# Forget gates of a decoder trunk: from 24 split products on 16 lanes to 32 single precision products in four column tiles

## The chip, the cores and the metric

The kernel runs on one core of a Trainium2 chip. A core has five engines that run their own instruction streams beside each other: PE (TensorE, matrix products into PSUM), DVE (VectorE), ACT (ScalarE), POOL (GpSimd) and SP (SyncE, which here only issues DMAs). PE's work shows as two kinds of records, loads of the stationary operand (PEld) and products (PE). The metric is the device time of one execution in microseconds; smaller is better.

## The reference, cut to what matters

The model is a trunk of two layers over 512 tokens of width 1024. Layer 0 is a dilated attention with a convolutional feed-forward network (FFN). After it, keys, values and one forget gate for each of 16 heads are projected once from the residual stream; layer 1 is a causal attention over them, with a bias made of the gates, and a second FFN. The gates are the part that the change touches:

```python
kvf = rms_norm(h, kv_norm) @ w_kvf                       # (1, 512, 2064)
k_sh = kvf[..., :B_WIDTH].reshape(B, T, B_HEADS, HEAD_DIM)
v_sh = kvf[..., B_WIDTH:2 * B_WIDTH].reshape(B, T, B_HEADS, HEAD_DIM)
log_f = jax.nn.log_sigmoid((kvf[..., 2 * B_WIDTH:] + b_f).astype(jnp.float32))
c_sh = jnp.cumsum(log_f, axis=1)                         # over the 512 tokens
...
s = s + (c_t[:, :, q0:q1, None] - c_t[:, :, None, :q1])  # in the cross attention
```

Everything is single precision (float32) and the result is compared at that precision. The gates are a product of 512 x 1024 by 1024 x 16, a bias, a log of a sigmoid, and a running sum over tokens.

## The kernel before

*Split products.* Nearly all products of the kernel are made of three: each float32 operand is split into a high part, rounded to the matrix engine's fast type float32r, and a low part, the rest; high by high, high by low and low by high are added up in PSUM (`mm3`, lines 263 to 266: L264, L265 and L266 are these three). The class `Weights` (L33) loads pieces of the weights through SP's queue (L47), rounds them on ACT (L55) and subtracts on DVE (L63); `W.get` hands out the next pair and splits a few pieces ahead of use.

*Layout.* Activations lie transposed: 128 of the 1024 features on the partitions, 8 chunks of them, and the 512 tokens along the free dimension. `SharedBoundary` (L432) stands between the FFN of layer 0 and the shared projections. For each block of 128 tokens it normalizes a row block, transposes it on PE (L468), scales it by the gain of `kv_norm` (L470, `gcol`), and keeps it three ways: `xT` high (L475, ACT) and low (L476, DVE), both scaled, and `nT` (L480, ACT), the transposed input without a gain, in float32. `second` (L486, L487) makes the queries' input from `nT` with the other gain.

*The stage around the gates.* The order of the instructions of each engine is the order in which the program issues them. After the first half of the values (`values`, `keep_values`) a loop over 8 chunks of 128 key features runs: `keys(c)` multiplies a weight piece by `xT` (24 products into `k_ps`), ACT keeps the high half (L1299), DVE the low (L1300); for the first four chunks two chunks of the queries' input are made as well. In the rounds 1 to 5 the loop also calls `next(gate)`, one step of the generator `gates`: round 1 issues the products and ACT's copy with the bias, rounds 2 to 4 the chain of the log of the sigmoid, round 5 the running sum `c8`. In round 6 SP writes `c8` to memory (`cd`), from which `load_ck` later reads it back, spread over the partitions. After the loop PE transposes `c8` (`cq_ps`), the second half of the values follows, and then the cross attention, whose biases POOL makes of `ck` and `cq`.

*The products of the gates.* The weights of the gates (1024 x 16) are loaded and split ahead of the first FFN, at L1274 to L1278, their bias at L1280. `gates` multiplies 16 columns of weights by 512 tokens, 8 chunks in three products each, into one PSUM bank of 16 partitions (`f_ps`); the chain runs on tiles of 16 partitions by 512 tokens.

*Column tiles.* PE's array has 128 columns, one for each output partition. A product with few columns can be put into a part of it; the partition at which its output begins says which. The cross attention's products with the values (L1537, `o_ps`) do so with two halves of 64, one for each head of a pair; the gates of before use the first 32 columns only.

Of the kernel before, what the change touches and what calls it, by code (L numbers as in the profile page):

```python
# [8 lines left out]
F32 = mybir.dt.float32  # L9
F32R = mybir.dt.float32r  # L10
BF16 = mybir.dt.bfloat16
AF = mybir.ActivationFunctionType
ALU = mybir.AluOpType

D = 1024
T = 512
NB = 4
KD = D // 128
# [79 lines left out]
def trunk_kernel(ctx, tc, x, norm_gains, w_qkv_a, w_o_a, w_q_b, w_o_b, kv_norm, w_kvf, b_f,  # L98
                 w_up, conv_w, conv_b, w_down, rope, out):
    nc = tc.nc  # L100
    act, dve, pool, pe, sp = nc.scalar, nc.vector, nc.gpsimd, nc.tensor, nc.sync
# [5 lines left out]
    sml = ctx.enter_context(tc.tile_pool(name="sml", bufs=6))  # L107
# [8 lines left out]
    def t2(shape, dt=F32, name="t2"):  # L116
        return p2.tile(shape, dt, tag="t2", name=name)

    def bank(shape, name="bank"):
        return psp.tile(shape, F32, tag="ps", name=name)  # L120
# [86 lines left out]
    def load_gain(src, name):  # L207
        t = t4([128, D], name=name)
        sp.dma_start(t, bass.AP(tensor=src.tensor, offset=src.offset, ap=[[0, 128], [1, D]]))
        return t  # L210
# [52 lines left out]
    def mm3(o, ah, al, bh, bl, first, last, shared=False):  # L263
        pe.matmul(o, ah, bh, start=first, stop=False, skip_group_check=shared)  # L264
        pe.matmul(o, ah, bl, start=False, stop=False, skip_group_check=shared)  # L265
        pe.matmul(o, al, bh, start=False, stop=last, skip_group_check=shared)  # L266
# [71 lines left out]
    def xs(xT, kc, s):  # L338
        return xT[0][kc // 4][:, kc % 4, s], xT[1][kc // 4][:, kc % 4, s]
# [8 lines left out]
    ALL, LO, HI = slice(0, 512), slice(0, 256), slice(256, 512)  # L348
# [909 lines left out]
    gcol = sml.tile([128, 16], F32, tag="gcol", name="gcol", bufs=1)  # L1258
# [13 lines left out]

    wf = t2([128, 8, 16], name="wf")
    sp.dma_start(wf, w_kvf[:, 2048:2064].rearrange("(k p) c -> p k c", p=128))  # L1274
    wfh = sml.tile([128, 8, 16], F32R, tag="wfh", name="wfh", bufs=1)
    wfl = sml.tile([128, 8, 16], F32R, tag="wfl", name="wfl", bufs=1)
    dve.tensor_copy(wfh, wf)
    dve.tensor_tensor(wfl, wf, wfh.bitcast(F32), ALU.subtract)  # L1278
    bfc = sml.tile([16, 1], F32, tag="bfc", name="bfc", bufs=1)
    sp.dma_start(bfc, b_f.rearrange("(p o) -> p o", o=1))  # L1280


    bd2 = SharedBoundary(load_gain(norm_gains[0, 3], "gain03"), gcol, "xk")
# [18 lines left out]
    c8 = t2([16, T], name="c8")  # L1302

    def gates():

        fo = bank([16, T], name="f_ps")
        for s in (ALL,):
            for kc in range(KD):
                bh, bl = xs(bd2.xT, kc, s)
                mm3(fo[:, s], wfh[:, kc, :], wfl[:, kc, :], bh, bl, kc == 0, kc == KD - 1)  # L1310

        z = t2([16, T], name="z")
        act.activation(z, fo, AF.Identity, bias=bfc)
        yield
        u = t2([16, T], name="u")
        e = t2([16, T], name="e")
        dve.tensor_scalar(u, z, -1.0, None, ALU.mult)
        dve.tensor_tensor(u, u, z, ALU.min)
        act.activation(e, u, AF.Exp)
        yield  # L1320
        dve.tensor_scalar(u, e, 1.0, None, ALU.add)
        dve.scalar_tensor_tensor(e, u, -1.0, e, ALU.add, ALU.subtract)
        dve.tensor_scalar(z, z, 0.0, None, ALU.min)
        lg = t2([16, T], name="lg")
        act.activation(lg, u, AF.Ln)
        dve.reciprocal(u, u)
        yield
        dve.tensor_tensor(e, e, u, ALU.mult)
        dve.tensor_tensor(lg, lg, e, ALU.subtract)
        dve.tensor_tensor(z, z, lg, ALU.subtract)  # L1330
        dve.memset(u, 1.0)
        yield
        dve.tensor_tensor_scan(c8, u, z, 0.0, ALU.mult, ALU.add)
        dve.tensor_scalar(c8, c8, 8.0, None, ALU.mult)
        yield

# [19 lines left out]
    first, second = bd2.order[:2], bd2.order[2:]  # L1356
    bd2.norm(second[1])
    gate = gates()
    banks = {b: bank([128, 512], name="v_ps") for b in bd2.order}
    wv = []  # L1360
# [115 lines left out]
    def f_scores(j, i0):  # L1476

        if i0 == 0:
            o = [bank([128, 2, 256], name="s_ps") for _ in range(2)]
            s = [[o[hh][:, i] for hh in range(2)] for i in range(2)]  # L1480
        else:
            s = [[bank([128, T], name="s_ps") for _ in range(2)] for _ in range(2)]
        q, k = query_parts(j), key_parts(j)
        for i in range(2):
            nn = max((i0 + i + 1) * 128, 256)
            qs = slice((i0 + i) * 128, (i0 + i + 1) * 128)
            for n, (a, b) in enumerate(((0, 0), (1, 0), (0, 1))):
                for hh in range(2):
                    rows = slice(64 * hh, 64 * hh + 64)
                    pe.matmul(s[i][hh][:, :nn], q[a][rows, qs], k[b][rows, :nn], start=n == 0, stop=n == 2)  # L1490
        return s
# [73 lines left out]
    for m in range(M + 2):  # L1565
        live = m < M
        if live:
# [3 lines left out]
            s = f_scores(j, i0)  # L1571
# [11 lines left out]
        for a in range(2):  # L1583
            i = i0 + a
# [72 lines left out]
```

## Time and profile before

| | us |
|---|---|
| median of 3 runs | 1122.44 |
| lowest and highest of them | 1122.23, 1122.62 |
| the profiled execution, its time | 1124.33 |
| the profiled execution, its span from first to last instruction | 1122.1 |
| granted clock of TensorE in it | 0.997 of full |

| stage | us from the span's start |
|---|---|
| gates' weights and bias issued on SP | 171 |
| first key product | 552 |
| products of the gates | 563.0 to 568.6 |
| ACT's copy of them with the bias | 568.8 |
| running sum `c8` done | 594.9 |
| first product of the cross attention with the values | 643.1 |

How to read the rows that follow: in the timeline the first two numbers are the start and the duration in us, then engine, line, operation, output<-inputs, shape and count; several of a kind in a row are merged into one, with the whole stretch as duration. For a product, "128*16" is rows by columns of the array in use, and "128x512" its streamed input, partitions by elements. Both float32 and float32r are written f32 there. In brackets stands how long the engine was idle before, and what ended that. SPq is SP's queue, where issues of DMAs stand. In views by line, three numbers with slashes are the least, median and greatest duration in ns. In a view of windows, the busy us of PE, PEld, DVE, ACT and POOL follow with their counts, then the granted clock, the share of the DMA engines and GB/s.

### The profile page before, as it was taken

What the parts mean: (1) busy time and instruction counts of PE and PEld (TensorE: products, weight loads), DVE (VectorE), ACT (ScalarE), POOL (GpSimd) and SP (SyncE); (2) the same over time, 40 slices, a digit from 0 to 9 for tenths busy, and PEclk for the clock granted to TensorE, in tenths of its full rate; (3) what the DMA queues carried; (4) which work ended last, traced back from release to release, by engine and by line L of the source; (5) the groups of instructions that cost most, each with busy time, mean ns of one, the idle gap of its engine ahead of it and who ended that gap; (6) DMA issues with size and microseconds to landing.
All of it is one profiled execution on the core that took longest, in us unless ns stands there. A gap on an engine that the chain in (4) does not pass through costs nothing.

```text
span 1122.1 us, 17314 instructions
## 1 busy us (share of the span) xinstructions
PE 1111.5 (99%) x6331; PEld 946.1 (84%) x6331; DVE 876.5 (78%) x1433; ACT 606.2 (54%) x1022; POOL 181.1 (16%) x275
## 2 busy tenths in 40 slices
PE   9999999999999999999999999999999999999997
PEld 6988789989989988888878788889989989988886
DVE  6667778888888589897576766848888888599894
ACT  5444466445445457576452577856445445457572
POOL 1832000300000121000000555500300000121000
PEclk9999999999999999999999999999999999999999
DMA  9469864334444599884447744364334444599862
GB/s 323 151 218 406 319 171 121 107 95 123 126 127 123 144 353 379 309 311 120 131 150 237 232 116 114 96 208 117 109 95 122 123 131 123 143 354 367 323 244 76
DMA packets 178191, 214.20 MB, mean 191 GB/s; under 512 B 11001, under 2 KB 130793, under 8 KB 178106
## 3 DMA queue, kind: packets, MB, share of 16 engines
q1 hardware_dynamic: 168634, 180.84, 49.0%
q0 software_dynamic: 9472, 32.25, 9.1%
q8 instruction: 50, 0.82, 0.3%
q14 instruction: 35, 0.29, 0.1%
HBM read 166.08 MB, written 39.63 MB: 183 GB/s over the span
## 4 chain that ended last, share of the span: by engine, by line
PE 96%; DVE 2%; ACT 1%; issue 0%; DVEq 0%; ACTq 0%
PE up L265 13%; PE up L264 13%; PE up L266 13%; PE acc L264 8%; PE acc L265 8%; PE acc L266 8%; PE v_ps L264 2%; PE v_ps L266 2%; PE v_ps L265 2%; PE qk_ps L264 2%; PE qk_ps L265 2%; PE qk_ps L266 2%; PE o_ps L1537 2%; PE s_ps L1490 2%; PE pT_ps L1522 2%; PE q_ps L264 2%
## 5 line engine op out<-in xcount | busy, mean ns | idle before, releaser
L63 DVE TENSOR_TENSOR w<-wraw,w 128x1024 fp32r<-128x1024 f32 x96 | 123.4, 1313 | 26.3 <-ACT w L55 25.7
L593 ACT ACTIVATE bb<-up,conv 128x512 f32<-128x512 f32 x80 | 60.6, 776 | 149.2 <-DVE up L918 76.2
L55 ACT CAST w<-wraw 128x1024 fp32r<-128x1024 f32 x110 | 111.9, 1048 | 21.7 <-PE v_ps L265 11.6
L264 PE MATMUL acc<-w 128*128 128x512 f32 (+1 forms) x311 | 120.6, 388 | 1.1 <-DVE mix L311 1.1
L266 PE MATMUL acc<-w 128*128 128x512 f32 (+1 forms) x311 | 120.4, 387 | 0.0
L264 PE MATMUL up<-xbh,w 128*128 128x512 f32 (+1 forms) x292 | 104.8, 359 | 0.0
L265 PE MATMUL up<-xcl,w 128*128 128x512 f32 (+1 forms) x292 | 104.8, 359 | 0.0
L264 PE MATMUL up<-xch,w 128*128 128x512 f32 (+1 forms) x292 | 104.8, 359 | 0.0
L265 PE MATMUL up<-xbl,w 128*128 128x512 f32 (+1 forms) x292 | 104.8, 359 | 0.0
L266 PE MATMUL up<-xch,w 128*128 128x512 f32 (+1 forms) x292 | 104.7, 358 | 0.0
L266 PE MATMUL up<-xbh,w 128*128 128x512 f32 (+1 forms) x292 | 104.7, 358 | 0.0
L265 PE MATMUL acc<-w 128*128 128x512 f32 (+1 forms) x267 | 103.2, 387 | 0.0
L609 POOL DMA_DIRECT2D hD<-hc x42 | 24.2, 577 | 319.7 <-DVE hc L611 316.5
L264 PEld LDWEIGHTS acc<-w 128*128 128x128 f32 x311 | 58.4, 188 | 13.2 <-DVE mix L311 1.3
L266 PEld LDWEIGHTS acc<-w 128*128 128x128 f32 x311 | 58.4, 188 | 12.0
L594 DVE SCALAR_TENSOR_TENSOR bb<-up,conv,bb 128x511 f32<-128x511 f32 x80 | 59.4, 743 | 7.8 <-ACT bb L593 7.8
L264 PE MATMUL up<-xsh,w 128*128 128x256 f32 x224 | 63.4, 283 | 0.0
L265 PE MATMUL up<-xsl,w 128*128 128x256 f32 x224 | 63.4, 283 | 0.0
L266 PE MATMUL up<-xsh,w 128*128 128x256 f32 x224 | 63.4, 283 | 0.0
L264 PEld LDWEIGHTS up<-xch,w 128*128 128x128 f32 x292 | 55.1, 189 | 8.3
L264 PEld LDWEIGHTS up<-xbh,w 128*128 128x128 f32 x292 | 55.1, 189 | 8.3
L596 DVE SCALAR_TENSOR_TENSOR bb<-up,conv,bb 128x510 f32<-128x510 f32 x80 | 59.9, 749 | 2.8
(301 smaller groups left out, 2991.2 us busy)
## 6 DMA issues: line engine op xcount, KB each, us to landing
wraw<-in_w_up_dram SPq DMA_DIRECT2D x88, 512.0 KB, 4.8
dT<-dsums SPq DMA_DIRECT2D x24, 512.0 KB, 6.6
dsums<-in_w_down_dram SPq DMA_DIRECT2D x22, 512.0 KB, 7.6
dsums<-in_w_down_dram SPq DMA_DIRECT2D x44, 256.0 KB, 7.0
hD<-hc POOLq DMA_DIRECT2D x44, 256.0 KB, 4.7
dact<-hD SPq DMA_DIRECT2D x44, 256.0 KB, 6.6
wraw<-dT SPq DMA_DIRECT2D x22, 512.0 KB, 9.1
wraw<-in_w_down_dram SPq DMA_DIRECT2D x22, 512.0 KB, 6.0
```

What stands on the lines that cost most here:

```text
L55: self.nc.scalar.copy(pair[:, 0], raw)
L63: self.nc.vector.tensor_tensor(pair[:, 1], raw, pair[:, 0].bitcast(F32), ALU.subtract)
L264: pe.matmul(o, ah, bh, start=first, stop=False, skip_group_check=shared)
L265: pe.matmul(o, ah, bl, start=False, stop=False, skip_group_check=shared)
L266: pe.matmul(o, al, bh, start=False, stop=last, skip_group_check=shared)
L593: act.activation(bb[:, s, :], ps, AF.Identity, bias=cp[:, 3, ch:ch + 1], scale=cp[:, 2, ch:ch + 1])
L594: dve.scalar_tensor_tensor(bb[:, s, 1:], ps[:, :T - 1], cp[:, 1, ch:ch + 1], bb[:, s, 1:], ALU.mult, ALU.add)
L596: dve.scalar_tensor_tensor(bb[:, s, 2:], ps[:, :T - 2], cp[:, 0, ch:ch + 1], bb[:, s, 2:], ALU.mult, ALU.add)
L609: pool.dma_start(hD[c - 1], hc.pop(c - 1))
L1490: pe.matmul(s[i][hh][:, :nn], q[a][rows, qs], k[b][rows, :nn], start=n == 0, stop=n == 2)
L1522: pe.transpose(o[:, k0 + k, :], p[:, hh, k * 128:(k + 1) * 128], ident)
L1537: pe.matmul(o[64 * hh:64 * hh + 64, i * 128:(i + 1) * 128], Vt[hd // 8][:, k, (hd % 8) * 64:(hd % 8) * 64 + 64], pT[j, i, hh][:, k, :], st ...
```

## The change

The products of the gates are made in plain float32 instead of three float32r products. The gain is multiplied into the gates' weights once, ahead of the first FFN, so that the products read `nT`, the input without a gain. The 512 tokens are cut into quarters of 128; each quarter's product writes its own 32 partitions of one PSUM tile of 128 x 128 (`fo`), that is, its own column tile, with 16 heads and 16 columns of zeros. The chain then runs on 128 x 128 instead of 16 x 512, in four parts of one tile `zt`; the last subtraction is made quarter by quarter and brings the tokens back to 16 x 512 (`zz`) for the running sum. The bias is loaded four times, once for each quarter, into a column that POOL has cleared, and POOL clears the weights' tile as well.

```diff
@@ -1272,12 +1272,13 @@
 
     wf = t2([128, 8, 16], name="wf")
     sp.dma_start(wf, w_kvf[:, 2048:2064].rearrange("(k p) c -> p k c", p=128))
-    wfh = sml.tile([128, 8, 16], F32R, tag="wfh", name="wfh", bufs=1)
-    wfl = sml.tile([128, 8, 16], F32R, tag="wfl", name="wfl", bufs=1)
-    dve.tensor_copy(wfh, wf)
-    dve.tensor_tensor(wfl, wf, wfh.bitcast(F32), ALU.subtract)
-    bfc = sml.tile([16, 1], F32, tag="bfc", name="bfc", bufs=1)
-    sp.dma_start(bfc, b_f.rearrange("(p o) -> p o", o=1))
+    wfg = sml.tile([128, 8, 32], F32, tag="wfg", name="wfg", bufs=1)
+    pool.memset(wfg, 0.0)
+    dve.tensor_tensor(wfg[:, :, 0:16], wf, gcol[:, 0:8, None].to_broadcast([128, 8, 16]), ALU.mult)
+    bfc = sml.tile([128, 1], F32, tag="bfc", name="bfc", bufs=1)
+    pool.memset(bfc, 0.0)
+    for q in range(4):
+        sp.dma_start(bfc[32 * q:32 * q + 16], b_f.rearrange("(p o) -> p o", o=1))
 
 
     bd2 = SharedBoundary(load_gain(norm_gains[0, 3], "gain03"), gcol, "xk")
@@ -1303,17 +1304,16 @@
 
     def gates():
 
-        fo = bank([16, T], name="f_ps")
-        for s in (ALL,):
-            for kc in range(KD):
-                bh, bl = xs(bd2.xT, kc, s)
-                mm3(fo[:, s], wfh[:, kc, :], wfl[:, kc, :], bh, bl, kc == 0, kc == KD - 1)
-
-        z = t2([16, T], name="z")
+        fo = bank([128, 128], name="f_ps")
+        for kc in range(KD):
+            for q in range(4):
+                pe.matmul(fo[32 * q:32 * q + 32], wfg[:, kc, :],
+                          bd2.nT[kc // 4][:, kc % 4, q * 128:q * 128 + 128], start=kc == 0, stop=kc == KD - 1)
+
+        zt = t2([128, 4, 128], name="z")
+        z, u, e, lg = (zt[:, i] for i in range(4))
         act.activation(z, fo, AF.Identity, bias=bfc)
         yield
-        u = t2([16, T], name="u")
-        e = t2([16, T], name="e")
         dve.tensor_scalar(u, z, -1.0, None, ALU.mult)
         dve.tensor_tensor(u, u, z, ALU.min)
         act.activation(e, u, AF.Exp)
@@ -1321,16 +1321,18 @@
         dve.tensor_scalar(u, e, 1.0, None, ALU.add)
         dve.scalar_tensor_tensor(e, u, -1.0, e, ALU.add, ALU.subtract)
         dve.tensor_scalar(z, z, 0.0, None, ALU.min)
-        lg = t2([16, T], name="lg")
         act.activation(lg, u, AF.Ln)
         dve.reciprocal(u, u)
         yield
         dve.tensor_tensor(e, e, u, ALU.mult)
         dve.tensor_tensor(lg, lg, e, ALU.subtract)
-        dve.tensor_tensor(z, z, lg, ALU.subtract)
-        dve.memset(u, 1.0)
+        zz, one = t2([16, T], name="zz"), t2([16, T], name="one")
+        for q in range(4):
+            r = slice(32 * q, 32 * q + 16)
+            dve.tensor_tensor(zz[:, q * 128:q * 128 + 128], z[r], lg[r], ALU.subtract)
+        dve.memset(one, 1.0)
         yield
-        dve.tensor_tensor_scan(c8, u, z, 0.0, ALU.mult, ALU.add)
+        dve.tensor_tensor_scan(c8, one, zz, 0.0, ALU.mult, ALU.add)
         dve.tensor_scalar(c8, c8, 8.0, None, ALU.mult)
         yield
 
```

## Prediction

> **What bounds the kernel now.** I read the page first: the span, the busy shares and the shares of the chain of waits; then the list of PE's waits from the gates to the end.
>
> ```profile
> span 1122.1 us, 17314 instructions
> PE 1111.5 (99%) x6331; PEld 946.1 (84%) x6331; DVE 876.5 (78%) x1433; ACT 606.2 (54%) x1022; POOL 181.1 (16%) x275
> PE 96%; DVE 2%; ACT 1%; issue 0%; DVEq 0%; ACTq 0%
> PE acc L264 <- DVE mix L311: 1.1, 1, 1.1
> ```
>
> PE is busy throughout and is 96% of the chain that ends last. A busy PE is not by itself a full PE, so the last row matters more: it is the whole list of what PE waited for from 563 us to the end, one wait of 1.1 us. After the gates PE is fed without a break, so a microsecond that PE no longer needs there should leave the end, as long as nothing that feeds it falls behind.
>
> The gates' place on PE, from the timeline, and the busy time of the engines between their first product and the next key tile's:
>
> ```profile
> 562.80 0.39 PE L266 MATMUL k_ps<-xkh,w 128*128 128x512 f32 x1
> 562.80 0.09 PEld L264 LDWEIGHTS f_ps<-xkh,wfh 128*16 128x16 f32 x1
> 563.02 0.39 PE L264 MATMUL f_ps<-xkh,wfh 128*16 128x512 f32 x1
> 563.26 0.40 PE L265 MATMUL f_ps<-xkl,wfh 128*16 128x512 f32 x1
> ...
> 568.35 0.40 PE L266 MATMUL f_ps<-xkh,wfl 128*16 128x512 f32 x1
> 568.59 0.40 PE L264 MATMUL k_ps<-xkh,w 128*128 128x512 f32 x1
> 563.02:568.59 5.57, 5.57 (x26) 2.38 (x24) 5.47 (x9) 1.82 (x3) 1.07 (x2) 1.00 0.92 296
> ```
>
> A matmul's 0.39 us is its latency; what it costs is the distance to the next start, 0.23 us. The 24 products of the gates hold PE from 563.02 to 568.59, 5.57 us at a granted clock of 1.00, with 16 of 128 columns in use. Entering and leaving them costs nothing: 0.22 and 0.24 us, as between any two.
>
> **What the change puts there.** 32 calls (8 chunks, 4 quarters) in plain single precision, 128 tokens each, the quarters in four column tiles of 32. The trace has no four column tiles, but it has two, in the cross attention's products with the values (o_ps), whose calls also stream 128 columns in single precision. Behind them stand four transposes, of the same streaming length on the whole array:
>
> ```profile
> L1537 PEld LDWEIGHTS o_ps<-pT,Vt x320: 132/137/137, 643.1 to 737.9; 128*64 128x64 f32 x160
> L1537 PE MATMUL o_ps<-pT,Vt x320: 272/273/323, 643.1 to 738.0; 128*64 128x128 f32 x160
> 700.57 1.04 PE L1490 MATMUL s_ps<-kst,qst 64*128 64x384 f32 x8
> 701.53 1.75 PE L1537 MATMUL o_ps<-pT,Vt 128*64 128x128 f32 x28
> 701.53 1.51 PEld L1537 LDWEIGHTS o_ps<-pT,Vt 128*64 128x64 f32 x28 [0.36 <-issue]
> 703.21 0.50 PE L264 MATMUL q_ps<-xqh,w 128*128 128x512 f32 x1
> 703.55 0.39 PE L265 MATMUL q_ps<-xql,w 128*128 128x512 f32 x1
> ...
> 693.38 0.60 PE L1522 MATMUL pT_ps<-ident,bias 128*128 128x128 f32 x4
> ```
>
> Three readings. First, a single precision call leaves two records: the loops at L1537 make 8 x (1+2+3+4) x 2 = 160 calls and there are 320 records. The change therefore issues 64 loads and 64 products in place of 24 and 24. Second, one such record holds its tile for 0.11 us: the four transposes' starts span 0.60 - 0.27 = 0.33 us, three steps. Third, two column tiles run side by side: 28 records start within 1.75 - 0.27 = 1.48 us, 0.055 us apart on average, which is 14 records in each tile at 0.11. Their loads (137 ns each) lie in the same 1.5 us, so they are hidden behind products.
>
> If four tiles run side by side as two do, each takes 8 calls x 2 records x 0.11 = 1.76 us. Around o_ps the change of tiling shows: the last s_ps product starts at 701.22 (700.57 + 1.04 - 0.39), o_ps follows 0.31 later where 0.23 is usual; the last o_ps starts at 703.01 and q_ps follows after 0.20 instead of 0.11, its second product after 0.34 instead of 0.23. Together 0.3 us. The gates of before already sit in a corner of the array and pay nothing. So 0 to 0.3 us; I take 0.2, nearer to the rows that really move between column tiles. New cost 1.96 us, saved 5.57 - 1.96 = 3.6 us.
>
> The bounds of this term: with only two tiles at a time 64 x 0.055 = 3.5 us plus 0.3, saved 1.8; one at a time 64 x 0.11 = 7.0 plus 0.3, lost 1.8; all four and no switch, saved 3.8. I take four because the two in the rows are at the full rate of each.
>
> A rule speaks against the even division. The Trainium skill, "TensorE: Matmul & The Clock Gate", Part 3, gives a speedup of 2.38 for three column tiles, not 3. Estimated from that page, four tiles at the same efficiency would be worth 3.2, the products 2.2 us and the time 1119.3; two tiles in this trace show no such loss (0.055 is half of 0.11).
>
> **The other parts.** They are meant to lie beside PE; here is their cover.
>
> ```profile
> 170.96 0.37 SPq L1274 DMA_DIRECT2D wf<-in_w_kvf_dram  x1
> 171.37 0.57 SPq L1280 DMA_DIRECT2D bfc<-in_b_f_dram  x1
> 174.92 0.34 SPq L209 DMA_DIRECT2D gain<-in_norm_gains_dram  x1
> 140.48 2.54 POOL L1078 COPY fac<-f_f 128x1024 f32<-128x1024 f32 x2 [26.66 <-DVE f_f L1075]
> 195.31 10.20 POOL L628 TENSOR_TENSOR xsum<-xbh,xbl 128x2048 f32<-128x2048 f32 x2 [52.30 <-DVE xbl L336]
> 545.57 1.07 ACT L480 COPY nT<-xt_ps 128x512 f32<-128x512 f32 x2
> 584.04 3.33 DVE L1326 RECIPROCAL u<-u 16x512 f32<-16x512 f32 x1
> 587.31 1.15 DVE L63 TENSOR_TENSOR w<-wraw,w 128x1024 fp32r<-128x1024 f32 x1
> 589.68 0.68 DVE L1329 TENSOR_TENSOR lg<-lg,e 16x512 f32<-16x512 f32 x1
> 590.59 0.59 ACT L1299 CAST kst<-k_ps 128x512 fp32r<-128x512 f32 x1 [3.91 <-PE k_ps L266]
> 591.55 1.15 DVE L63 TENSOR_TENSOR w<-wraw,w 128x1024 fp32r<-128x1024 f32 x1
> 596.02 0.59 ACT L1299 CAST kst<-k_ps 128x512 fp32r<-128x512 f32 x1 [3.91 <-PE k_ps L266]
> ```
>
> *Bias and weights.* Three more small loads on SP's queue are 1.7 us at 0.57; the queue stands from 171.9 to 174.92 before its next issue. The first of them waits for POOL's clearing of bfc; behind it on SP stand the gain03 load and the w_up pieces. POOL runs dry at 143.0 and has nothing until 195.31, so both clearings (256 and 1 elements a row) are long done by 171. On DVE two short operations become one; the gates' weights are then idle for almost 400 us. Cost nothing. If POOL were late, SP would hold up w_up pieces by as much; its 52 us of idle time exclude that.
>
> *The first product's waits.* It reads nT instead of the split input: ACT's last copies end at 546.6, 16 us ahead. It also waits for POOL's clearing, past. The first value product later waits in addition for an older product of PE itself, long past too.
>
> *The chain of the gates.* The operations keep their order among DVE's and ACT's but stream 128 columns on 128 lanes instead of 512 on 16. No row gives a 128-wide reciprocal; from above it is 3.33 us as now, from below a quarter, 0.8. The others are bounded likewise by their 512-wide rows, such as 0.68. The subtraction that becomes four quarters adds at most 3 x 0.68 = 2.0 us to DVE and likely nothing (four times a quarter of the columns). Who waits: the low halves of key weights 6 and 7 stand behind the chain on DVE. Weight 6 is ready at 588.46 and its products follow those of key 5, which ACT's cast marks at 590.59: 2 us of slack. Weight 7 is ready at 592.70 against 596.02: 3.3 us. Both ends move earlier with PE, since DVE's stretch begins with a wait for PE's key tiles; with a shorter reciprocal the slack grows to 4 us or more, and even if nothing shortened and the 2.0 us came on top, weight 7 would have 1.3 left. Cost nothing; a gain neither, as PE does not wait there now.
>
> **Sum.** The profiled execution took 1124.33 us (span 1122.1, 2.2 us around it); with 3.6 less it is 1120.7. The median of the runs shown, 1122.44, lies 1.9 below the profiled execution; from it the forecast is 1118.8.
>
> **Rivals.**
>
> 1. *The tiles share more than the array.* The densest stretch in the rows above is 28 loads and 28 products in 1.5 us, 27 ns for each PE instruction. Four tiles want 128 instructions in 1.76 us, half of that. If 27 ns is a limit of issue, or of how fast the input can be read, the block is 3.5 us plus up to 0.3: time 1120.6, in a milder form 1119.5 to 1120.6. For it: no denser stretch is in these rows. Against: nothing in them waits for issue, each tile is simply full. Beside it: the same page of the Trainium skill, Part 1, states that starts of matmuls never come closer than about 25 ns; four starts per 0.11 us would just clear that, and no run here shows it.
>
> 2. *No overlap at all*, because both records of a call go to the same tile and PE takes them in order: 7.0 + 0.3 us, 1124.2. The o_ps rows, made of the same pairs, speak against it.
>
> 3. *Slower: loads in the open.* Each of the 64 records brings a load, 94 ns for 16 columns and 137 for 64.
>
> ```profile
> L264 PEld LDWEIGHTS f_ps<-xkh,wfh x8: 94/94/98, 562.8 to 567.7; 128*16 128x16 f32 x8
> ```
>
> If a load cannot run beside a product in another column tile, 64 x (0.11 + 0.094 to 0.137) = 13.1 to 15.8 us replace 5.57: 1130 to 1132.7. It decides as soon as a record costs over 5.57 / 64 = 0.087 us. The Trainium skill, "TensorE: Matmul & The Clock Gate", Part 3, states it as a rule: a load overlaps products in flight only if their row groups differ, which column tiles never do. The o_ps rows, with 28 loads inside the stretch of 28 products at 0.055 us each, contradict it.
>
> 4. *The saving is lost downstream*, key weights 6 and 7 or the value weights then ending last: 1122.4. The slack above speaks against it.
>
> **How the numbers follow.** Forecast 0.62 (own range 1118.2 to 1119.4), rival 1 0.22, rival 2 0.05, rival 3 0.06, rival 4 0.05. No change means within 0.2%, 2.2 us, which is what a measurement of this kernel can tell: 1120.2 to 1124.7. Faster is the forecast and the mild quarter of rival 1, 0.67; within is the rest of rival 1, with rivals 2 and 4, 0.26; slower is rival 3, a little widened by what no row shows, 0.07. The range 1118.0 to 1121.0 holds forecast and rival 1, 0.84: its low end is a free switch (1118.6) with half a microsecond for the rest, its high end two tiles at a time with the dearer switch (1120.7).
>
> **What would show it.** In the profile after, 64 records of 32 columns write f_ps, in clusters of four starts 0.11 us apart, and the next key product starts about 1.9 to 2.1 us after the first of them. Clusters of two mean rival 1, singles rival 2, starts over 0.087 us apart rival 3. PE's list of waits after the gates stays at the 1.1 us of L264; a new entry with DVE's w would mean rival 4. The reciprocal should be near 0.8 us, key weight 6 over 4 us early. The forecast is wrong above all if the time of the four-tile block is not that of its fullest tile.

## The result and the profile after

| | before | after |
|---|---|---|
| median of the executions of the comparison (22 each), us | 1122.59 | 1120.16 |
| their range, us | 1122.14 to 1124.76 | 1119.10 to 1122.32 |
| profiled execution, us | 1124.33 | 1120.19 |

The ratio of after to before is 0.9977, 95% interval 0.9971 to 0.9984: faster by 2.4 us, where 3.6 were forecast. The time lies inside the range of the prediction and 1.4 us above its centre, but outside the 1118.2 to 1119.4 that the prediction gave to its own mechanism.

The page of the changed kernel, its span, its busy shares and its chain of waits:

```profile
span 1118.4 us, 17405 instructions
PE 1106.8 (99%) x6371; PEld 943.9 (84%) x6371; DVE 872.9 (78%) x1435; ACT 606.0 (54%) x1022; POOL 181.7 (16%) x277
...
PE 90%; DMA 5%; DVE 2%; ACT 1%; issue 1%; SPq 0%; DVEq 0%; ACTq 0%
PE up L264 12%; PE up L265 12%; PE up L266 12%; PE acc L264 8%; PE acc L266 8%; PE acc L265 8%; DMA dsums<-in_w_down_dram 3%; PE v_ps L266 2%; PE v_ps L264 2%; PE v_ps L265 2%; PE o_ps L1539 2%; PE s_ps L1492 2%; PE pT_ps L1524 2%; PE qk_ps L265 2%; PE qk_ps L266 2%; PE q_ps L264 2%
```

PE is busy 4.7 us less: the gates need less of it, and the profile of before has a slow stretch that this one has not (below). But its share of the chain went from 96% to 90%, and a transfer is on the chain that was not there: a load of `w_down` for the sums (`dsums`). How far that load is the cause is weighed below. The list of PE's waits (wait, total, times, longest) names the place; three of its rows:

```profile
PE acc L264 <- DVE mix L311: 1.1, 1, 1.1
PE qk_ps L265 <- DVE w L63: 1.0, 2, 0.8
PE acc L266 <- DVE w L721: 0.6, 1, 0.6
```

The first two are in the list of before too. The third is new, and it lies in the second FFN, 446 us behind the gates.

The gates themselves, first their instructions as a group (durations least, median, greatest; first and last start), then PE's timeline around them:

```profile
L1310 PEld LDWEIGHTS f_ps<-nT,wfg x64: 106/110/110, 561.7 to 563.3; 128*32 128x32 f32 x64
L1310 PE MATMUL f_ps<-nT,wfg x64: 272/273/297, 561.7 to 563.4; 128*32 128x128 f32 x64
```

```profile
561.40 0.39 PE L266 MATMUL k_ps<-xkh,w 128*128 128x512 f32 x1
561.72 1.69 PEld L1310 LDWEIGHTS f_ps<-nT,wfg 128*32 128x32 f32 x64 [0.35 <-issue]
561.72 1.96 PE L1310 MATMUL f_ps<-nT,wfg 128*32 128x128 f32 x64
563.60 0.50 PE L264 MATMUL k_ps<-xkh,w 128*128 128x512 f32 x1
563.94 0.40 PE L265 MATMUL k_ps<-xkl,w 128*128 128x512 f32 x1
```

64 records, as counted in the prediction. The single starts inside the merged row, read from the same trace, come in clusters of four:

```
561.718 .725 .732 .738 | 561.852 .858 .865 .872 | 561.961 .967 .974 .981 | ... | 563.380 .387 .393 .400
```

Four starts lie 7 ns apart and the clusters 0.109 us: four column tiles run side by side, each at its own full rate. The block takes 563.60 - 561.72 = 1.88 us.

To see where the time went, the starts of the same products in the two traces were matched in order, and the steps in their difference listed:

| at, us before | step, us | what lies there |
|---|---|---|
| 122 to 126 | -1.35 | value products of the first attention, at half clock in the profile of before alone |
| 563 to 569 | -3.59 + 0.10 = -3.48 | the gates' products, with the switch back |
| 1013 (1009 after) | +0.73 + 0.11 = +0.84 | second FFN, the new wait |
| elsewhere | -0.07 | |

Together -4.06; the times of the two executions differ by 4.14. The first row is not the change's. The granted clock is the last number but two in a window's row, here of before and, in the second fence, of after:

```profile
122.50:125.70 3.20, 3.20 (x11) 2.63 (x11) 3.10 (x12) 3.20 (x16) 0.00 (x0) 0.54 1.00 386
```

```profile
122.50:125.70 3.20, 3.20 (x18) 2.66 (x17) 3.10 (x15) 3.20 (x17) 0.00 (x0) 1.00 1.01 379
```

After a wait of 1.24 us at 120 us (`s_ps` for the DVE copy `qkT`, in both kernels), the clock falls to half for some 3 us in some executions of either kernel, which is a good part of the spread of the times in the first table. So of the change itself the two profiles show -3.48 + 0.84 = -2.64 us, close to the 2.4 of the medians.

The third row. VectorE (DVE) on the timeline of the second FFN, before (the first fence) and after (the second):

```profile
994.15 0.69 DVE L560 TENSOR_TENSOR dsums<-dsums 128x512 f32<-128x512 f32 x1
994.88 0.69 DVE L561 TENSOR_TENSOR dsums<-dsums 128x512 f32<-128x512 f32 x1
995.60 0.69 DVE L562 TENSOR_TENSOR dsums<-dsums 128x512 f32<-128x512 f32 x1
...
1005.36 0.42 DVE L708 TENSOR_TENSOR dact<-dact 128x256 f32<-128x256 f32 x1 [1.65 <-DMA dact<-hD]
...
1010.48 1.22 DVE L721 TENSOR_TENSOR w<-dact,w 128x1024 fp32r<-128x1024 f32 x1
```

```profile
990.13 0.69 DVE L560 TENSOR_TENSOR dsums<-dsums 128x512 f32<-128x512 f32 x1 [0.95 <-DMA dsums<-in_w_down_dram]
990.86 0.69 DVE L561 TENSOR_TENSOR dsums<-dsums 128x512 f32<-128x512 f32 x1
993.03 0.69 DVE L562 TENSOR_TENSOR dsums<-dsums 128x512 f32<-128x512 f32 x1 [1.48 <-DMA dsums<-in_w_down_dram]
...
1001.05 0.43 DVE L707 TENSOR_TENSOR dact<-dact 128x256 f32<-128x256 f32 x1 [0.44 <-DMA dact<-hD]
1002.81 0.42 DVE L708 TENSOR_TENSOR dact<-dact 128x256 f32<-128x256 f32 x1 [1.33 <-DMA dact<-hD]
...
1007.93 1.22 DVE L721 TENSOR_TENSOR w<-dact,w 128x1024 fp32r<-128x1024 f32 x1
```

Before, the four subtractions of the last `w_down` pair (L559 to L562; the last three are shown) run without a gap. After, two of them stand 0.95 and 1.48 us for pieces of the pair that have not landed. But this is not the last wait on the way. About 9 us later VectorE stands for a second load, `dact`, in both kernels: 1.65 us before, 0.44 and 1.33 us after. From L708 on it works without a gap to the low halves for the down products (L721), which end 6.34 us behind the start of L708 before and 6.33 us after. So the landing of `dact` sets L721. Its load was issued at 985.17 us (L701 on SP's queue), ahead of the two stalls, so they did not hold it up; had the pair landed in time, these rows say, VectorE would have stood the longer for `dact`.

Both loads are late in the same way. A load reports its landing in sixteen updates of a semaphore, which the trace keeps. After, the last update of the second piece of `dact` comes 3.2 us behind the fifteenth (1002.72 and 999.51 us), and that of the pair's last piece 4.7 us (992.93 and 988.23). Before, the same two lag by 2.1 and 2.5 us.

L721 ends at 1009.15 in place of 1006.75, where PE's lead of 4.95 us at this point would put it (1011.70 - 4.95). PE, on its timeline:

```profile
1008.24 0.39 PE L265 MATMUL acc<-w 128*128 128x512 f32 x1
1009.20 0.50 PE L266 MATMUL acc<-w 128*128 128x512 f32 x1 [0.57 <-DVE w L721]
1009.53 0.39 PE L264 MATMUL acc<-w 128*128 128x512 f32 x1
```

In before this product starts at 1013.41, 1.71 us behind the end of L721's row: that was the slack, and 2.4 us of lateness uses it up and leaves 0.7. The restart after the wait costs 0.11 more.

### The profile page after: what moved, and what is told of

Read it like the earlier page. It is cut to its first block, busy times and chain, and to the rows that moved or that the text cites. A ratio compares the mean times of both kernels' runs of the same rounds, so it can differ in the third digit from the quotient of the medians.

```text
span 1118.4 us, 17405 instructions
## 1 busy us (share of the span) xinstructions
PE 1106.8 (99%) x6371; PEld 943.9 (84%) x6371; DVE 872.9 (78%) x1435; ACT 606.0 (54%) x1022; POOL 181.7 (16%) x277
## 4 chain that ended last, share of the span: by engine, by line
PE 90%; DMA 5%; DVE 2%; ACT 1%; issue 1%; SPq 0%; DVEq 0%; ACTq 0%
PE up L264 12%; PE up L265 12%; PE up L266 12%; PE acc L264 8%; PE acc L266 8%; PE acc L265 8%; DMA dsums<-in_w_down_dram 3%; PE v_ps L266 2%; PE v_ps L264 2%; PE v_ps L265 2%; PE o_ps L1539 2%; PE s_ps L1492 2%; PE pT_ps L1524 2%; PE qk_ps L265 2%; PE qk_ps L266 2%; PE q_ps L264 2%
```

## Experiments

Four sets; the kernels of a set ran on one chip. Theory at the start: the products save what was forecast, and the new wait takes about 1 us of it back. The rival: the wait has nothing to do with the change, or comes of PE's being earlier alone, so that any saving at the gates loses as much. If it belongs to the change, the question is to which part of it.

### First set: repeat, and one part at a time

The changed kernel again, unaltered:

> The changed kernel once more, to see whether what its first profile showed comes back: the block of the gates 1.88 us long, 3.5 us shorter than before with its entry and exit, and a wait of PE for DVE's w (0.6 us) near 1008 us, in the hand-over from the up to the down products of the second FFN. Theory A (this wait is part of the price of an earlier PE or of something else in the change): a wait of that kind is there again, the stretch from the gates' end to the program's end is about 1 us longer than the 553.3 us of before, and the time is about 1120.1. Theory B (chance of one execution): no such wait, the stretch is 553.3 us again, and the time is 1119.0.

Median 1120.69 of 7 (1118.80 to 1121.71), ratio 0.9974 (0.9964 to 0.9985). Its profile has the gates' step of -3.48 again, no wait at L721, and the half clock at 123 us (0.66). So the saving on PE is fixed, and the wait is not in every execution. VectorE does not stand for the pair here, and yet L721 ends only 0.63 us ahead of its product, where before had 1.71: `dact` is late (L708 stands 1.85 us for it).

The products before, with two of the three products of each chunk left out:

```
-                mm3(fo[:, s], wfh[:, kc, :], wfl[:, kc, :], bh, bl, kc == 0, kc == KD - 1)
+                pe.matmul(fo[:, s], wfh[:, kc, :], bh, start=kc == 0, stop=kc == KD - 1)
```

> The kernel before with the high-by-high products of the gates alone: 8 of the 24 products remain, 16 are left out (the low parts take no part), and nothing else is touched. PE's block falls from 5.57 to 8 x 0.232 = 1.86 us, 3.7 us saved, about as much as the change saves. If an earlier PE by itself costs about 1 us later on, the time is 1122.5 - 3.7 + 1.0 = 1119.8; if the change loses it through something else (its three more loads on SP's queue, its other chain), the full 3.7 arrive: 1118.8.

Median 1118.98 of 5, ratio 0.9963 (0.9950 to 0.9977); the gates' step is -3.71, and nothing is given back later. In this profile PE's being earlier does not by itself bring the wait.

The kernel before with three more small loads of the bias on SP's queue:

```
+    bfx = sml.tile([16, 3], F32, tag="bfx", name="bfx", bufs=1)
+    for q in range(3):
+        sp.dma_start(bfx[:, q:q + 1], b_f.rearrange("(p o) -> p o", o=1))
```

> The kernel before with three more small loads of the bias behind the first one, into a tile that nobody reads: the same number of DMAs on SP's queue as the changed kernel, and PE's work unchanged. My prediction costs them at nothing: 1122.5. If the later loads come out differently because of them (SP's loads take turns on eight semaphores, and three more shift all later ones), a loss of up to 1 us: 1123.5.

Median 1122.79 of 11, ratio 0.9994 (0.9985 to 1.0003): the loads cost nothing that this measurement can tell, as predicted.

Single precision in one column tile, 512 tokens a call:

```
+        for kc in range(KD):
+            pe.matmul(fo, wfg[:, kc, :], bd2.nT[kc // 4][:, kc % 4, :], start=kc == 0, stop=kc == KD - 1)
```

> The single precision products on the unscaled input, but all 512 tokens in one column tile of 16 columns, 8 calls, with the chain on 16 x 512 as before and one load of the bias: the change without its column tiles. By the rows of before (a single precision record holds its tile for 0.11 us for each 128 columns) the 16 records take 16 x 0.437 = 7.0 us in place of 5.57, so 1.4 us slower than before: 1123.9. If single precision were not the dearer form in one tile, the time would be that of before or less.

Median 1124.17 of 11, ratio 1.0005 (0.9996 to 1.0014), too near to tell; the trace tells. Its PE timeline:

```profile
561.71 7.04 PE L1306 MATMUL f_ps<-nT,wfg 128*16 128x512 f32 x16
568.68 0.50 PE L264 MATMUL k_ps<-xkh,w 128*128 128x512 f32 x1
```

The block is 568.68 - 561.71 = 6.97 us where 5.57 stood, and the step against before is +1.50, then +0.10 on the next product. The change to single precision by itself loses; the tiles turn 6.97 us into 1.88.

### Second set: the half clock taken out, and the chain's form

To measure one microsecond, the wait at 120 us was taken out of all four kernels of this set: two of the copies there run on ACT.

```
-        dve.tensor_copy(qkT[g][:, b], o)
+        (act.copy if (g, b) in ((2, 2), (2, 3)) else dve.tensor_copy)(qkT[g][:, b], o)
```

The kernel before with this line alone:

> The kernel before with one line changed: ACT instead of DVE copies the last two transposed key and query blocks (L999) in the first attention, to take away a nuisance of the comparison. In the executions so far PE waits there 1.24 us for DVE (from 119.8 us on) and in some of them, of either kernel, the granted clock then falls to 0.54 for the next 3 us, which costs 1.4 to 1.6 us more; the times fall into two groups some 1.9 us apart. If the wait is what brings the fall, the wait shrinks by about 1.2 us, the clock stays at 1.00 in every execution, and the times form one group near 1121.3 (1122.5 less the wait). If the fall has nothing to do with the wait, two groups remain.

The changed kernel with it:

> The changed kernel with the same line. Against the kernel before with that line it should show the gain without the nuisance: 3.5 us less if nothing is lost later (theory B of the first run: the wait near 1008 us is chance), 2.5 us less if the change brings the loss of about 1 us with it (theory A). With 1121.3 for the kernel before this is 1117.8 or 1118.8; it would be the fastest kernel of the study.

The kernel with a third of the products, with it:

> The kernel before with one third of the gates' products (16 of 24 left out, the low parts take no part) and the same line. PE alone is shortened, by 3.7 us. Theory A with the cause in the change's other parts: 3.7 less than the kernel before with that line, and 1.2 us faster than the changed kernel with it. Theory B: 3.7 less, and within 0.2 to 0.3 of the changed kernel, which is the difference of the two blocks (3.7 against 3.5).

The changed kernel with it, and with the chain of the gates on 16x512 as before: four copies on ACT bring the quarters back behind each other, and the chain's lines are those of before.

```
-        act.activation(z, fo, AF.Identity, bias=bfc)
+        z = t2([16, T], name="z")
+        for q in range(4):
+            r = slice(32 * q, 32 * q + 16)
+            act.activation(z[:, q * 128:q * 128 + 128], fo[r], AF.Identity, bias=bfc[r])
```

> The changed kernel with the same line and the chain of the gates on 16 x 512 again: ACT copies the four quarters out of the column tiles one by one, and DVE's chain is that of before, its reciprocal at 3.33 us. By my prediction the chain lies beside PE in either form: the time is that of the changed kernel with that line (within 0.3 us). If the shorter chain is what keeps the weights of keys 6 and 7 in time, PE waits there for DVE's w, up to 1.5 us, and the time is longer by that.

| kernel with the copy on ACT | median, us (range) | step at the gates | wait at L721 |
|---|---|---|---|
| before | 1121.21 (1120.68 to 1121.90) | | none |
| changed | 1119.02 (1118.71 to 1119.51) | -3.48 | 0.6 us, step +0.84 |
| a third of the products | 1117.55 (1117.50 to 1117.58) | -3.71 | none |
| changed, chain on 16x512 | 1117.83 (1117.67 to 1118.26) | -3.48 | none |

No profile of this set has the wait at 120 us, and in the three looked at there (before, changed, and late_sums_128 below) the granted clock is 1.00 in that stretch. The spread of the times shrinks to about 1 us. The second and the last row differ only in the chain, and the last is 1.2 us faster: against before with the same line, the products are worth 1121.21 - 1117.83 = 3.4 us when nothing is given back. It is also the fastest kernel of this set that computes everything. In its profile VectorE stands 0.91 us for the last piece of the pair too, and 1.25 us at L708; L721 still ends 0.49 us ahead of its product, so PE does not wait.

Outside the chain, the order of the instructions of every engine and their waits are the same in these two. They differ in two things: the chain's own instructions, and the number of tiles that the gates take from the ring of eight `t2` tiles, five in the changed kernel and six in the other, so that all later `t2` tiles lie one place apart.

### Third set: the places in the ring, swapped

The changed kernel with six tiles, and chain16_act with five:

```
-        z, u, e, lg = (zt[:, i] for i in range(4))
+        (z, _, e, lg), u = (zt[:, i] for i in range(4)), t2([128, 128], name="u")
```

```
-        lg = t2([16, T], name="lg")
+        lg = c8
```

> The changed kernel with the one-line copy move of before_act, chain on 128x128; only u now has a tile of its own in the ring of eight t2 tiles, so that the gates take six of them from the ring, as in before.py, and not five. Every later t2 tile (hc, dt, dsum, pT) then lies where it lies in before.py; the order and the waits of all engines stay those of after_act (1119.02 there). Theory A, the place of the later tiles in the ring is what makes VectorE late at the second FFN's hand-over: the wait acc L266 <- DVE w L721 of 0.6 us is gone and the time is that of chain16_act, 1117.8 (1117.3 to 1118.4). Theory B, the chain's own instructions shift the later work: the wait stays and the time is 1119.0 (1118.6 to 1119.6). Theory C, the wait comes and goes with no fixed cause in the program: no prediction, between 1117.7 and 1119.1.

> chain16_act (column-tile products, chain back on 16x512, the copy move) with lg in c8's tile, so that the gates take five tiles of the ring and not six; order and waits of all engines stay those of chain16_act (1117.83 there), and every later t2 tile lies where it lies in after.py. Theory A (place in the ring): the wait acc L266 <- DVE w L721 of 0.6 us appears and the time is 1119.0 (1118.6 to 1119.6). Theory B (the chain's own instructions): no such wait, 1117.8 (1117.3 to 1118.4). Theory C (no fixed cause): between 1117.7 and 1119.1, in no relation to the number of tiles.

With six tiles and the chain on 128x128: 1118.08, 1118.19, 1118.77, 1119.02, 1119.29. With five tiles and the chain on 16x512: 1117.85, 1117.86, 1117.92, 1118.12, 1119.69. Theory A has fallen: the places did not move the loss to the other kernel. And the loss is not fixed to a program: the first kernel's times lie in two groups, and the second's one high time stands alone. Counting the executions above 1118.5 us: with the chain on 128 lanes 8 of 10 (after_act and tiles128_six), with the chain on 16 lanes 1 of 13 (chain16_act, chain16_five, third_act). The chain's form seems to shift how often the loss comes; it does not decide it. This is theory B as a matter of odds, and a weak one: the limit of 1118.5 was chosen with the times in view, third_act makes fewer products, and in the third set alone it is 3 of 5 against 1 of 5, so the odds rest on after_act against chain16_act, 5 of 5 against 0 of 4.

The profiles show the same mechanism as in the changed kernel. VectorE in tiles128_six, an execution of 1119.29 us, and in chain16_five, one of 1117.86:

```profile
989.23 0.69 DVE L560 TENSOR_TENSOR dsums<-dsums 128x512 f32<-128x512 f32 x1 [1.29 <-DMA dsums<-in_w_down_dram]
...
991.95 0.69 DVE L562 TENSOR_TENSOR dsums<-dsums 128x512 f32<-128x512 f32 x1 [1.30 <-DMA dsums<-in_w_down_dram]
...
1001.90 0.43 DVE L708 TENSOR_TENSOR dact<-dact 128x256 f32<-128x256 f32 x1 [1.45 <-DMA dact<-hD]
```

```profile
987.76 0.69 DVE L560 TENSOR_TENSOR dsums<-dsums 128x512 f32<-128x512 f32 x1
...
989.21 0.69 DVE L562 TENSOR_TENSOR dsums<-dsums 128x512 f32<-128x512 f32 x1
...
999.63 0.43 DVE L708 TENSOR_TENSOR dact<-dact 128x256 f32<-128x256 f32 x1 [1.50 <-DMA dact<-hD]
```

L721 ends at 1008.24 and 1005.97 us, 6.34 us behind the start of L708 in both: again `dact` sets it. In all twelve profiles of kernels with the subtractions in their old place L708 stands for `dact`. L721 ends 1.5 to 2.5 us ahead of its product in the six profiles without four column tiles, 0.5 to 1.0 us ahead in three with them (after_again, chain16_act, chain16_five), and 0.7 to 1.0 us too late in the three that lose (after, after_act, tiles128_six).

The issue of the last piece of that pair on SP's queue, in the same two executions:

```profile
976.61 0.33 SPq L556 DMA_DIRECT2D dsums<-in_w_down_dram  x1
```

```profile
978.86 0.33 SPq L556 DMA_DIRECT2D dsums<-in_w_down_dram  x1
```

The piece that was issued 2.2 us earlier is the one that VectorE waits for. Fifteen of its sixteen updates were there earlier too (by 986.87 us against 988.08); the last came 3.3 us later (991.85 against 988.55). In this stretch the DMA engines have nothing left (the last two numbers are their share and GB/s):

```profile
976.00:992.00 16.00, 16.00 (x72) 13.28 (x71) 12.99 (x23) 10.25 (x13) 4.94 (x8) 1.00 1.05 321
```

```profile
976.00:992.00 16.00, 16.00 (x72) 13.28 (x71) 15.48 (x27) 10.03 (x13) 5.81 (x10) 1.00 1.05 328
```

Both kernels, tiles128_six first, move data at about the same full rate; what differs is how far one part of each load lags behind the others.

### Fourth set: take VectorE out from behind the load

The theory that this set tests: if the wait for that pair is the whole of the loss, its cure is there and not at the gates. The four subtractions and their store go one place later, in the second FFN only:

```
-                    if c == NF - 2:
+                    if c == NF - 2 and s <= 1 - l:
                         next(sums)
...
+                        if l and c == NF - 1:
+                            next(sums)
                         if c >= NF - 2:
                             pair_highs(c - NF + 2)
```

> after_act (chain on 128x128, copy move), and in the second FFN the four subtractions of the last w_down pair (L559 to L562) with their store go one place later on VectorE, behind the low parts and the second tap of the chunk that follows, so that VectorE no longer stands still behind the pair's load at 987 to 992 us. Theory A, the late load of that pair is what makes VectorE late for the hand-over at 1008 us: no wait acc L266 <- DVE w L721, 1117.8 (1117.3 to 1118.3) in nearly every round, 1.2 below after_act. Theory B, the loads are late as a whole and VectorE is then held by dact<-hD at 997 to 1002 us as before: the wait stays, 1118.5 to 1119.5 in most rounds. Theory C, the four subtractions come in the way at the new place, right ahead of the hand-over: 1119.5 to 1121 with a longer wait at L721.

> chain16_act (chain on 16x512, copy move) with the same four subtractions one place later. Theory A: 1117.8 (1117.3 to 1118.3) without the rare round above 1119, the same as late_sums_128, since the wait was the only thing that the chain's form decided. Theory B: 1117.8 again, but 1 us below late_sums_128. Theory C: slower than 1119, with the wait at L721.

Medians of 5: 1118.16 (1117.90 to 1118.69) with the chain on 128x128 and 1118.04 (1117.77 to 1118.21) on 16x512. The 1.2 us between the two forms of the chain are gone (0.12 is left, with overlapping ranges), one of ten executions is above 1118.5, and neither profile has the wait at L721. VectorE in late_sums_128:

```profile
997.32 0.69 DVE L562 TENSOR_TENSOR dsums<-dsums 128x512 f32<-128x512 f32 x1
997.93 0.42 DVE L707 TENSOR_TENSOR dact<-dact 128x256 f32<-128x256 f32 x1
998.38 0.42 DVE L708 TENSOR_TENSOR dact<-dact 128x256 f32<-128x256 f32 x1
...
1003.50 1.22 DVE L721 TENSOR_TENSOR w<-dact,w 128x1024 fp32r<-128x1024 f32 x1
```

The subtractions now fill the time in which VectorE used to stand for `dact`, and L721 ends at 1004.72; the product that needs it starts at 1006.74, so there are 2.0 us of slack. The times are those of theory A: with the four subtractions moved, the loss is gone from most executions. That the pair's load was the cause is not shown by this. In both profiles the last update of the pair's last piece and of `dact` comes at most 1.2 us behind the fifteenth, so neither profile has a lagging load that VectorE survived. L721 still ends 6.3 us behind L708, which needs `dact`, so a `dact` as late as in tiles128_six would still make PE wait. And the move also puts the pair's two stores of 512 KB some 8.5 us later, to about the landing of `dact` at 998.2 us, so that they are no longer in flight beside it. Fewer transfers beside `dact` may be what helps, and not VectorE's order; no run tells the two apart. No kernel without the move but with the copy on ACT ran on this chip. Against before on the same chip the ratios are 0.9951 (0.9938 to 0.9963) and 0.9950 (0.9936 to 0.9963), with the copy on ACT in them. The kernels of the four sets that compute everything and do not have the loss lie between 1117.8 and 1118.2, about 2 us below the changed kernel; that is partly the copy on ACT, which is no part of the change.

## Why the prediction was nearly right, and where it was not

*What bounds the kernel.* Right: PE was earlier by 3.48 us after the gates and stayed so for 440 us, and in the profiles without the wait at L721 to the end.

*The block on PE.* Right in its mechanism, short by 0.1 in one term. Forecast: 16 records a tile at 0.11 and 0.2 us for the change of tiling, saved 3.6. Measured: 16 x 0.109 = 1.74, and for the switch 0.09 on entering (561.72 - 561.40 = 0.32 where 0.23 is usual), 0.09 on leaving (563.60 - 563.40 = 0.20 where 0.11 is usual) and 0.10 on the next product, 0.3 in all. That was the upper bound, read from the o_ps rows; taking a value below the rows cost 0.1 us.

*Rivals 1 to 3.* All fell. Four starts stand in 0.109 us, so 27 ns for each instruction was the tiles' own pace and no limit of issue (the block has 128 instructions in 1.74 us, 14 ns each). The 64 loads of 106 to 110 ns lie in the same 1.69 us as the products. Here the trace differs from the Trainium skill, "TensorE: Matmul & The Clock Gate", Part 3, which lets a load overlap only products of other row groups: these loads, all of one row group, lie beside the products all the same. The gates of before, on all rows too, already had 2.38 us of loads inside their 5.57 us of products. The same page of the Trainium skill, Part 3, gives 2.38 for three column tiles, where four turned one tile's 6.97 us into 1.88 here, 3.7 times with the switch and 4.0 without it. The same page of the Trainium skill, Part 1, has no two starts closer than about 25 ns, which does not hold between column tiles, where these are 7 ns apart.

*The other parts at nothing.* The loads cost nothing that a run could tell (more_loads). The chain went as argued: the reciprocal took 0.95 us where about 0.8 was expected, the four subtractions 1.16, and key weight 6 was ready at 580.46, 5.2 us ahead of the cast that ends key 5's products (over 4 expected). VectorE and ACT of the changed kernel:

```profile
578.29 0.95 DVE L1325 RECIPROCAL z<-z 128x128 f32<-128x128 f32 x1 [0.22 <-ACT z L1324]
579.23 1.23 DVE L63 TENSOR_TENSOR w<-wraw,w 128x1024 fp32r<-128x1024 f32 x1
582.13 1.16 DVE L1332 TENSOR_TENSOR zz<-z 16x128 f32<-16x128 f32 x4
```

```profile
585.69 0.59 ACT L1300 CAST kst<-k_ps 128x512 fp32r<-128x512 f32 x1 [3.90 <-PE k_ps L266]
```

*The step that failed* is "Cost nothing" of the chain, together with the place of rival 4. Cover was looked for where the chain runs, at key weights 6 and 7 and the value weights, and it was there. The loss came 440 us later, at the hand-over of the second FFN, where VectorE had 1.7 us of slack behind the load of `dact`. Against PE that load landed 2.4 us later in the profile of after than in that of before (L708 starts 5.65 us ahead of the product in place of 8.05). Rival 4 had the kind (saving lost downstream to VectorE's `w`) and a chance of 0.05, but the wrong place, and it took the whole saving where about a quarter to a third was lost. The rows for it were in the trace of before: L559 to L562 run there with no wait, but the DMA engines were just as full (982 to 998 us before: share 1.05, 323 GB/s), and 9 us later on VectorE an operation on `dact` already stood 1.65 us for its load. That was the row to follow to L721 and its 1.7 us.

*The range.* That the time fell into it was in part luck. The forecast's own part was 1118.2 to 1119.4, and 1120.16 lies above it, in the part that was there for rival 1, two tiles at a time, which the trace refutes; it was mostly the loss in the second FFN, with a chance of 0.05 and another place and size in the prediction, that put it there. And "faster" came true by 0.04 us, against the prediction's limit of 1120.2.

*What stays open.* Why one part of the loads lags further in some executions, and why it seems to do so more often with the chain on 128 lanes. PE's lead alone does not bring it (third_act has as much), nor do the three loads alone (more_loads), and the places of the tiles did not move it to the other kernel. What is left are the change's own instructions and their times, on PE and in the chain on VectorE and ACT at 564 to 588 us, and no step was found that carries them to the transfers at 970 us. Nor do 23 executions make the odds exact. Open too is by which way the move of the fourth set helps.

## What to carry to other kernels

Narrow products (16 or 32 columns) that stream many tokens pay for the tokens, not for the columns: cut the tokens into quarters and give each a column tile, and even single precision, which alone is slower than three split products, comes out at a third of the time. A microsecond taken from a saturated engine can shift everything behind it against the transfers; before costing "the rest" at nothing, list the slacks of the feeding engine to the end of the kernel, above all where it runs in order behind a load in a stretch in which the DMA engines are full. Follow the waits to the last one ahead of the hand-over before naming the load that causes a loss. It can be met where the feeding engine waits (here, by moving four operations and their stores), and a loss that comes in some executions only is seen when another source of spread has been taken out first.

## What was not expected of the hardware

- One wait of 1.24 us on PE was followed, in some executions, by some 3 us at half the clock (0.54 in before's window of 122.5 to 125.7 us, 0.66 in one profile of the changed kernel, 1.00 in another with the same wait). It cost 1.35 us in the profile of before. With the wait removed the kernel before was at 0.9982 (0.9973 to 0.9991) of its time.
- Four column tiles lose nothing to each other: 7 ns between the starts of neighbours and 0.109 us between clusters, the same as one tile alone takes for 128 columns of single precision.
- With the DMA engines full, a load that was issued 2.2 us earlier was the one that landed too late, by the last of its sixteen updates alone: 5.0 us behind the fifteenth in tiles128_six, 0.5 us in chain16_five.
